# First 256 MLP channels with the tokens stationary, the second tile's root from sums, and boundary adaLN units moved into the MLPs

## The chip, the core and the metric

One core of one Trainium2 chip runs the whole kernel. The metric is device time in microseconds (us), as the median of the runs shown. Engines are named as in the profile: PE multiplies, DVE is the vector engine, ACT the scalar engine, POOL a third engine for small work, SP issues most DMAs.

## The reference, cut to what matters

256 tokens of width 1024 pass four layers. Each layer is a token mixer (attention, convolution, pooling, attention) and then an MLP of 4096 channels. Each of these eight sub-layers does

```python
h = rmsnorm(x, g_pre) * (1 + sc) + sh
y = mixer(h)      # or: square(relu(h @ w1)) @ w2
x = x + gt * rmsnorm(y, g_post)
```

where `sc`, `sh` and `gt` come from `mod = silu(c) @ ada_w[i] + ada_b[i]`, six vectors of 1024 per layer. All is float32, and the products must be good to more than one pass of the fast matmul format.

## The kernel before

**Precision.** Each operand of a large product is split into two planes in the format fp32r: `hi` is the value rounded by ACT (L173 for weights), `lo = value - hi` by DVE (L174). `mm3` (L557, L560, L561) multiplies hi by hi, hi by lo and lo by hi. Weights arrive in tiles of 128x1024 (512 KB): five raw buffers, six `hi` and six `lo` buffers. SP issues their DMAs in the order of the program and waits there when no buffer is free.

**Tokens.** There are two tiles of 128 tokens, t = 0 and 1. The residual stream `xs` has tokens on partitions. Each sub-layer wants `h` transposed: the planes `hT_hi` and `hT_lo`, 128 channels on partitions, eight k by 256 tokens.

**MLP (`ffn`).** There are 16 blocks of 256 channels. For block c, `colblock` multiplies with the weights stationary and all 256 tokens moving (48 matmuls of 128x256 into one PSUM bank); ACT and DVE take relu, square and split it (L609 to L614), and `rowblock` adds its share of `w2` into four banks `y` (24 matmuls of 128x512), one block behind. The last two blocks go tile by tile, t = 0 first.

**Boundary (`boundary`).** Between two sub-layers, for each tile: squares of y (ACT), y times its gain (`y_scaled`, L496), the root (sum and power, L117 to L121, the power on POOL), `residual` (L501), squares of the new x, the second root, scaling (L358 or L388), the transposes on PE, and the fill of the planes (L399, L401 for t = 1; L538, L539 for t = 0). For t = 0 the root goes into the transposes as a diagonal matrix `dg` (L371, L377); for t = 1 it goes into `xa` (L388) ahead of plain transposes (L395). The first two column tiles of `transposed1` are 256 wide, the third 512.

**What sets the order.** A scheduler of the language orders each engine but SP: of what is ready it takes what comes first in the program, and the order is then fixed. `line(engine, ins)` ties the instructions of a boundary into one fixed order on ACT and one on DVE, in program order. `after` keeps casts and subtractions of later weights behind the last fill of the planes (`gate["act"]`, `gate["dve"]`); `gate["free"]` = GFREE = 2 lets the first two loads pass, which are the two weight tiles of the next block 0. A read of a PSUM bank by DVE waits for ACT's read of it.

**adaLN units.** `ada_w` is read in units of 1 MB, 24 per layer. `ada(n)` takes the next n units, in an MLP on DVE (two passes of 128x1024 each, L220 or L222, summed over units and brought to PE by `ada_flush`), elsewhere on PE (L256). Tables `MIX` and `FF` give for each sub-layer: units in its steps, units in the boundary ahead of it, units fetched ahead at its end.

Of the kernel before, what the change touches and what calls it, by code (L numbers as in the profile page):

```python
# [51 lines left out]
def tile_trunk(ctx: ExitStack, tc: tile.TileContext, x, cT, pos, invf, ada_w, ada_bg,  # L52
# [54 lines left out]
    sm.tile([P, 40], F32, tag="align_s", name="align_s", bufs=1)  # L107
# [261 lines left out]
    def transposed0(xa, r):  # L369
        dg = tmp.tile([P, P], F32, tag="dg", name="dg")  # L370
# [40 lines left out]
    def start(hi, lo):  # L411
        def sums(t):
            ms = sm.tile([P, 2], F32, tag="ms", name="ms")
            for n in range(2):
# [89 lines left out]
    def boundary(ys, units, planes=None, tokens=None):  # L504
# [7 lines left out]
        residual(0, v0, rsqrt_eps(*cols(m0)))
        if final:
            nc.sync.dma_start(out[0], xs[:, 0])
        else:
            ms = squares(0)
            xa = scaled(0)
        y_squares(1, ys, 0, m1)
        if not final:
            r = rsqrt_eps(*cols(ms))  # L520
            if tokens is not None:
                tokens(xa, r)
            else:
                bs = transposed0(xa, r)
        v1 = [y_scaled(1, ys, 0)]
        y_squares(1, ys, 1, m1)
        r1 = rsqrt_eps(*cols(m1), eng=V)
        v1.append(y_scaled(1, ys, 1))
        if final:
# [771 lines left out]
```

## Time and profile before

| what | value |
|---|---|
| median of 3 runs | 1192.34 us (1192.28 to 1196.03) |
| profiled execution, its own time | 1196.1 us |
| its span, first to last instruction | 1194.3 us |
| mean granted clock of PE in it | 0.984 |
| PE, DVE, ACT, POOL busy | 1145.1, 843.7, 570.2, 51.9 us |
| instructions | 19384 |
| DMA | 290.13 MB, 243 GB/s on average |

The profiled execution lies at the upper end of the runs. Its time is 1.8 us longer than its span. Busy PE counts matmuls that overlap, so it says only where PE had nothing in flight.

### The profile page before, as it was taken

How to read it: one execution, taken by the hardware profiler on the slowest of the kernel's cores; microseconds unless marked ns; L12 is line 12 of the kernel's file. 1: busy time of each engine (PE TensorE's matmuls, PEld its weight loads, DVE VectorE, ACT ScalarE, POOL GpSimd, SP SyncE). 2: the span in 40 equal slices, each digit the busy share in tenths (PEclk: the TensorE clock that was granted, in tenths of full speed). 3: DMA queues.
4: the chain of work that ended last, by engine and by line, in shares of the span. 5: the costliest groups of instructions: out<-in, count | busy, mean ns of one | idle time of the engine just before them, and what ended most of it. 6: DMA issues, size and time to landing. Idle time of an engine off the chain costs nothing.

```text
span 1194.3 us, 19384 instructions
## 1 busy us (share of the span) xinstructions
PE 1145.1 (96%) x7678; PEld 972.0 (81%) x7678; DVE 843.7 (71%) x1141; ACT 570.2 (48%) x952; POOL 51.9 (4%) x120
## 2 busy tenths in 40 slices
PE   7899989999999999999999989999998999999997
PEld 4667779899878866989898778998967877999996
DVE  3699687877665665868877687777766986655554
ACT  3355564444453245635444463544445665544442
POOL 1000010000010011000000210000010001000000
PEclk9999989999999999999999989999998999999999
DMA  8868757677727785888795577788536432765650
GB/s 336 310 272 326 290 209 299 254 305 290 266 71 251 255 320 194 330 329 345 277 391 213 212 256 285 308 321 325 185 93 228 147 124 87 231 190 182 194 176 36
DMA packets 73390, 290.13 MB, mean 243 GB/s; under 512 B 9986, under 2 KB 15234, under 8 KB 61012
## 3 DMA queue, kind: packets, MB, share of 16 engines
q1 hardware_dynamic: 70484, 280.44, 64.6%
q0 software_dynamic: 2816, 8.46, 2.2%
q8 instruction: 60, 0.98, 0.3%
q14 instruction: 30, 0.25, 0.1%
HBM read 286.57 MB, written 2.29 MB: 242 GB/s over the span
## 4 chain that ended last, share of the span: by engine, by line
PE 58%; DMA 3%; ACT 3%; DVE 3%; issue 2%; POOL 2%; SPq 0%; POOLq 0%; DVEq 0%; ACTq 0%
PE y L557 8%; PE h L557 8%; PE y L560 8%; PE h L561 8%; PE y L561 8%; PE h L560 8%; PE dw_ps L964 2%; ACT junk L135 1%; PE adap L256 1%; PE pw L557 1%; PE pw L560 1%; PE pw L561 1%; POOL r L121 1%; PE s_ps L877 1%; PE hT_ps L395 1%
## 5 line engine op out<-in xcount | busy, mean ns | idle before, releaser
L174 DVE TENSOR_TENSOR lo<-raw,hi 128x1024 fp32r<-128x1024 f32 (+1 forms) x336 | 394.1, 1194 | 168.2 <-ACT hi L173 167.1
L173 ACT CAST hi<-raw 128x1024 fp32r<-128x1024 f32 (+1 forms) x336 | 339.7, 1030 | 278.8 <-PE h L560 123.2
L557 PE MATMUL h<-hT_hi,hi 128*128 128x256 f32 x1024 | 291.9, 285 | 0.0
L560 PE MATMUL h<-hT_lo,hi 128*128 128x256 f32 x1024 | 291.9, 285 | 0.0
L561 PE MATMUL h<-hT_hi,lo 128*128 128x256 f32 x1024 | 291.3, 284 | 0.0
L557 PEld LDWEIGHTS h<-hT_hi,hi 128*128 128x128 f32 x1024 | 198.0, 193 | 3.8 <-issue 0.8
L557 PE MATMUL y<-hi,gh 128*128 128x512 f32 x512 | 200.9, 392 | 0.0
L560 PE MATMUL y<-lo,gh 128*128 128x512 f32 x512 | 200.6, 392 | 0.0
L560 PEld LDWEIGHTS h<-hT_lo,hi 128*128 128x128 f32 x1024 | 198.0, 193 | 2.2
L561 PE MATMUL y<-hi,gl 128*128 128x512 f32 x512 | 199.8, 390 | 0.0
L561 PEld LDWEIGHTS h<-hT_hi,lo 128*128 128x128 f32 x1024 | 197.9, 193 | 0.8 <-issue 0.8
L222 DVE SCALAR_TENSOR_TENSOR acc<-araw,c_act,acc 128x1024 f32<-128x1024 f32 x98 | 120.5, 1279 | 0.0
L561 PEld LDWEIGHTS y<-hi,gl 128*128 128x128 f32 x512 | 96.1, 188 | 23.3 <-issue 2.5
L557 PEld LDWEIGHTS y<-hi,gh 128*128 128x128 f32 x512 | 96.4, 188 | 22.1 <-issue 3.4
L560 PEld LDWEIGHTS y<-lo,gh 128*128 128x128 f32 x512 | 96.4, 188 | 22.0 <-issue 4.2
L609 ACT ACTIVATE r<-h 128x512 f32<-128x512 f32 x64 | 38.0, 594 | 98.0 <-PE h L561 96.8
L612 DVE TENSOR_TENSOR r<-r 128x512 f32<-128x512 f32 x64 | 44.2, 690 | 40.5 <-ACT gh L611 40.5
L496 DVE TENSOR_TENSOR v<-y,bc_g 128x512 f32<-128x512 f32 x32 | 21.8, 687 | 37.0 <-ACT junk L135 24.8
L614 DVE TENSOR_TENSOR gl<-r,gh 128x512 fp32r<-128x512 f32 x64 | 44.2, 691 | 1.7
L611 ACT ACTIVATE gh<-r 128x512 fp32r<-128x512 f32 x64 | 40.6, 634 | 1.7
L256 PE MATMUL adap<-araw,c_act 128*32 128x512 f32 x224 | 34.7, 604 | 3.6 <-DMA araw<-in_ada_w_dram 3.4
L135 ACT ACTIVATE junk<-y 128x512 bf16<-128x512 f32 x32 | 18.9, 592 | 37.5 <-PE y L561 37.3
(255 smaller groups left out, 1466.6 us busy)
## 6 DMA issues: line engine op xcount, KB each, us to landing
raw<-in_w_dram SPq DMA_DIRECT2D x256, 512.0 KB
araw<-in_ada_w_dram SPq DMA_DIRECT2D x96, 1024.0 KB
raw<-in_w_pw_dram SPq DMA_DIRECT2D x24, 512.0 KB
raw<-in_w_o_dram SPq DMA_DIRECT2D x16, 512.0 KB
u<-ud SPq DMA_DIRECT2D x32, 132.0 KB
raw<-in_w_ukv_dram SPq DMA_DIRECT2D x8, 512.0 KB
bc_g<-rowd POOLq DMA_DIRECT2D x8, 512.0 KB, 5.2
bc_a<-rowd POOLq DMA_DIRECT2D x7, 512.0 KB, 4.4
```

What stands on the lines that cost most here:

```text
L135: return A.activation(junk[:, :src.shape[-1]], src, AF.Square, scale=1.0 / math.sqrt(n), accum_out=acc)
L173: put(A.copy(h, raw), "act")
L174: put(V.tensor_tensor(l, raw, h.bitcast(F32), op=ALU.subtract), "dve")
L222: V.scalar_tensor_tensor(acc, raw[:, sl], ck, acc, op0=ALU.mult, op1=ALU.add)
L256: mm = T.matmul(grp["pt"][32 * j:32 * j + 32, :], lhsT, raw[j // 2][:, HALF[j % 2]], start=first, stop=stop)
L557: mm = T.matmul(o, ah, bh, start=start, stop=False, skip_group_check=True)
L560: T.matmul(o, ah, bl, start=False, stop=False, skip_group_check=True)
L561: return T.matmul(o, al, bh, start=False, stop=stop, skip_group_check=True)
L609: A.activation(r, hb, AF.Relu)
L611: A.activation(gh, r, AF.Square)
L612: V.tensor_tensor(r, r, r, op=ALU.mult)
L614: gli = V.tensor_tensor(gl, r, gh.bitcast(F32), op=ALU.subtract)
```

## The change

The change has five parts.

1. `mlp_head`: block 0 of each MLP is computed with the tokens stationary and 256 channels of weights moving, one bank for each token tile, 24 matmuls each. The first tile's (`first(0)`) come in the program inside the boundary, after the first parts of the second tile's planes; the second tile's come at c = 0 in `ffn`. The result has tokens on partitions, so four transposes follow, and the split reads PSUM.
2. `root_ahead`: the sum of squares of the new x of t = 1 is x·x + 2 r x·v + r² v·v, where x·x is kept from the last boundary (`keep_squares`), x·v comes from two `tensor_tensor_reduce` (`cross`) and v·v from two squares on ACT. The squares of the new x now come after the planes, for the next boundary.
3. Order in the boundary: v of the second tile and its first cross product come ahead of the scaling of t = 0; both hi fills of t = 0 come ahead of the second residual, which is split in halves around the scaling of t = 1; the sum for the first root goes to DVE.
4. The adaLN units of the boundaries ahead of MLPs 0, 1 and 2 (1, 4 and 3 units) go to these MLPs' blocks.
5. `dg` has one buffer in place of two; `GFREE` holds only ahead of mixers, since the loads of block 0 come ahead of the boundary.

```diff
+    def keep_squares(t, ms):
+        xx[t] = sm.tile([P, 1], F32, tag="xx", name="xx", bufs=2)
+        G.tensor_scalar(xx[t], ms[:, 0:1], ms[:, 1:2], EPS, ALU.add, ALU.add)
...
-    def transposed1(r, hi, lo):
+    def transposed1(r, hi, lo, rest):
...
         for ks in ((0, 1), (2, 3), (4, 5, 6, 7)):
+            if ks[0] == 4:
+                rest()
...
+    def cross(t, v, n, prev):
+        sl, v = v
+        junk = tmp.tile([P, 512], BF16, tag="junk2", name="junk2", bufs=1)
+        acc = sm.tile([P, 1], F32, tag="xv", name="xv", bufs=4)
+        line("dve", V.tensor_tensor_reduce(out=junk, in0=v, in1=xs[:, t, sl], scale=2.0 / D,
+                                           scalar=prev, op0=ALU.mult, op1=ALU.add, accum_out=acc))
+        return acc
+
+    def root_ahead(t, r, xv, vv):
+        v2 = sm.tile([P, 1], F32, tag="v2s", name="v2s", bufs=2)
+        line("dve", V.tensor_tensor(v2, vv[:, 0:1], vv[:, 1:2], op=ALU.add))
+        a = sm.tile([P, 1], F32, tag="ra1", name="ra1", bufs=2)
+        line("dve", V.tensor_scalar(a, v2, r, xv, ALU.mult, ALU.add))
+        b = sm.tile([P, 1], F32, tag="rb1", name="rb1", bufs=2)
+        line("dve", V.tensor_scalar(b, a, r, xx[t], ALU.mult, ALU.add))
+        r2 = sm.tile([P, 1], F32, tag="r", name="r")
+        gate["pow"] = G.tensor_tensor(r2, b, mhalf, op=ALU.pow)
+        return r2
...
-        residual(0, v0, rsqrt_eps(*cols(m0)))
+        residual(0, v0, rsqrt_eps(*cols(m0), eng=V))
...
+        ms = squares(0)
+        r = rsqrt_eps(*cols(ms))
+        y_squares(1, ys, 0, m1)
+        v1 = [y_scaled(1, ys, 0)]
+        line("act", sq(v1[0][1], D, vv[:, 0:1]))
+        xa = tmp.tile([P, D], F32, tag="xa", name="xa")
+        for h in range(2):
+            line("dve", V.tensor_tensor(xa[:, HALF[h]], xs[:, 0, HALF[h]], bct["a"][:, HALF[h]],
+                                        op=ALU.mult))
+            if h == 0:
+                xv = cross(1, v1[0], 0, 0.0)
+        if tokens is not None:
+            tokens(xa, r)
+        else:
+            bs = transposed0(xa, r)
+        y_squares(1, ys, 1, m1)
+        v1.append(y_scaled(1, ys, 1))
+        r1 = rsqrt_eps(*cols(m1), eng=V)
+        line("act", sq(v1[1][1], D, vv[:, 1:2]))
+        xv = cross(1, v1[1], 1, xv)
...
         if tokens is None:
-            fill0(0)
-        ms = squares(1)
-        r = rsqrt_eps(*cols(ms), eng=V)
+            low = [fill0(h) for h in range(2)]
+        r = root_ahead(1, r1, xv, vv)
+        if tokens is None:
+            low[0]()
+        residual(1, v1[:1], r1)
         if tokens is not None:
+            residual(1, v1[1:], r1)
             tokens(scaled(1), r)
         else:
-            rest = transposed1(r, *planes)
+            rest = transposed1(r, *planes, lambda: residual(1, v1[1:], r1))
             next(rest)
-            fill0(1)
+            low[1]()
+            if first is not None:
+                first(0)
             for _ in rest:
                 pass
+        keep_squares(1, squares(1))
         gate["pool"] = gate["pow"]
-        gate["free"] = GFREE
+        gate["free"] = GFREE if first is None else 0
...
+    def mlp_head(i, h):
         hh, hl = h
+        parts = [load(w1[i, 0, p]) for p in range(2)]
+        banks = []
+
+        def tile_of(t):
+            ts = slice(t * P, (t + 1) * P)
+            b = bank("h", "h0")[:, 0:256]
+            banks.append(b)
+            n = 0
+            for low in (False, True):
+                for kk in range(KT):
+                    wh, wl = parts[kk // 4]
+                    c = slice(256 * (kk % 4), 256 * (kk % 4) + 256)
+                    for st, mv in ((hl, wh),) if low else ((hh, wh), (hh, wl)):
+                        T.matmul(b, st[:, kk, ts], mv[:, c], start=(n == 0), stop=(n == 3 * KT - 1),
+                                 skip_group_check=True)
+                        n += 1
+        return tile_of, banks
...
+                if c == 0:
+                    tile_of(1)
+                    g2 = bank("h", "gT")
+                    for t in range(NT):
+                        rt = r[:, 256 * t:256 * t + 256]
+                        A.activation(rt, banks[t], AF.Relu)
+                        V.tensor_tensor(rt, rt, rt, op=ALU.mult)
+                        for f in range(2):
+                            T.transpose(g2[:, 256 * f + P * t:256 * f + P * t + P],
+                                        rt[:, P * f:P * f + P], ident)
+                    A.copy(gh, g2)
+                    gli = V.tensor_tensor(gl, g2, gh.bitcast(F32), op=ALU.subtract)
...
-        0: ([1, 2, 1, 0, 2, 0, 3, 0, 2, 2, 0, 0, 0, 1, 0, 0], 1, 3),
-        1: ([1, 1, 0, 1, 2, 2, 1, 2, 2, 2, 1, 0, 0, 1, 0, 0], 4, 3),
-        2: ([0, 2, 0, 2, 0, 3, 1, 1, 2, 0, 2, 0, 1, 3, 0, 1], 3, 0),
+        0: ([0, 2, 2, 1, 2, 1, 2, 1, 2, 1, 0, 0, 0, 1, 0, 0], 0, 3),
+        1: ([0, 1, 2, 2, 2, 2, 1, 2, 2, 2, 2, 0, 0, 2, 0, 0], 0, 3),
+        2: ([0, 2, 2, 2, 1, 2, 1, 2, 2, 1, 2, 0, 1, 2, 0, 1], 0, 0),
...
+            first = mlp_head(i, (hi, lo)) if m else None
```

## Rows read from the trace of the kernel before

**Rows 1.** Page, part 1: busy us (share of the span) xinstructions
```profile
PE 1145.1 (96%) x7678; PEld 972.0 (81%) x7678; DVE 843.7 (71%) x1141; ACT 570.2 (48%) x952; POOL 51.9 (4%) x120
```

**Rows 2.** Waits of PE: who, waited for, us in total, times, longest
```profile
PE hT_ps L395 <- DVE xa L388: 11.8, 6, 2.8
...
PE hT_ps L377 <- ACT dg L371: 5.8, 2, 2.9
```

**Rows 3.** Windows, y's end to block 0's relu, MLPs 3, 1, 0, 2: PE, PEclk, DMA
```profile
999.60:1014.00 14.40, 11.85 (x76) 0.88 0.23 75
469.60:485.40 15.80, 12.99 (x108) 1.00 0.86 317
149.80:167.90 18.10, 13.23 (x85) 0.81 0.27 100
685.00:705.90 20.90, 16.77 (x101) 0.76 0.55 190
```

**Rows 4.** Timeline of DVE, boundary ahead of MLP 3: start us, us, what
```profile
994.97 0.69 DVE L496 TENSOR_TENSOR v<-y,bc_g 128x512 f32<-128x512 f32 x1 [2.09 <-ACT junk L135]
996.06 1.41 DVE L501 SCALAR_TENSOR_TENSOR xs<-v,r,xs 128x512 f32<-128x512 f32 x2 [0.39 <-POOL r L121]
...
999.13 0.69 DVE L496 TENSOR_TENSOR v<-y,bc_g 128x512 f32<-128x512 f32 x1 [0.46 <-ACT junk L135]
1000.54 0.21 DVE L117 TENSOR_SCALAR v<-msy 128x1 f32<-128x1 f32 x1 [0.71 <-ACT junk L135]
...
1002.74 0.68 DVE L539 TENSOR_TENSOR hT_lo<-hT_ps,hT_hi 128x512 fp32r<-128x512 f32 x1
...
1004.65 1.54 DVE L388 SCALAR_TENSOR_TENSOR xa<-xs,r,bc_a 128x256 f32<-128x256 f32 x3 [0.66 <-POOL r L121]
1006.11 0.60 DVE L401 SCALAR_TENSOR_TENSOR hT_lo<-hT_ps,shc,hT_hi 128x128 fp32r<-128x128 f32 x2
...
1008.62 1.13 DVE L401 SCALAR_TENSOR_TENSOR hT_lo<-hT_ps,shc,hT_hi 128x128 fp32r<-128x128 f32 x4 [0.73 <-ACT hT_hi L399]
1009.67 4.62 DVE L174 TENSOR_TENSOR lo<-raw,hi 128x1024 fp32r<-128x1024 f32 x4
```

**Rows 5.** Timeline of ACT, the same boundary
```profile
999.53 0.40 ACT L371 ACTIVATE dg<-ident,r 128x128 f32<-128x128 f32 x1 [0.43 <-POOL r L121]
...
1003.02 0.63 ACT L135 ACTIVATE junk<-xs 128x512 bf16<-128x512 f32 x1
...
1007.45 1.14 ACT L399 ACTIVATE hT_hi<-hT_ps,shc 128x128 fp32r<-128x128 f32 x4 [0.27 <-PE hT_ps L395]
1008.46 4.85 ACT L173 CAST hi<-raw 128x1024 fp32r<-128x1024 f32 x5
```

**Rows 6.** Timeline of POOL, the same boundary: the power of the first root
```profile
995.45 0.57 POOL L121 TENSOR_TENSOR r<-v,mhalf 128x1 f32<-128x1 f32 x1
```

**Rows 7.** Timeline of DVE: last fills of the second tile, MLPs 0, 1 and 2
```profile
162.88 1.13 DVE L401 SCALAR_TENSOR_TENSOR hT_lo<-hT_ps,shc,hT_hi 128x128 fp32r<-128x128 f32 x4 [0.73 <-ACT hT_hi L399]
...
481.02 1.13 DVE L401 SCALAR_TENSOR_TENSOR hT_lo<-hT_ps,shc,hT_hi 128x128 fp32r<-128x128 f32 x4 [0.35 <-ACT hT_hi L399]
...
699.92 1.13 DVE L401 SCALAR_TENSOR_TENSOR hT_lo<-hT_ps,shc,hT_hi 128x128 fp32r<-128x128 f32 x4 [0.72 <-ACT hT_hi L399]
```

**Rows 8.** Timeline of DVE, boundary ahead of MLP 0: the first v
```profile
148.98 1.29 DVE L496 TENSOR_TENSOR v<-y,bc_g 128x512 f32<-128x512 f32 x2 [7.70 <-DMA bc_g<-rowd]
```

**Rows 9.** Timeline of DVE, boundary into pooling: tokens of the second tile
```profile
673.16 1.41 DVE L1105 SCALAR_TENSOR_TENSOR xa<-xa,r,shb 128x512 f32<-128x512 f32 x2
```

**Rows 10.** Timeline of PE, boundary ahead of MLP 1: units, then the first tile's products
```profile
469.53 3.64 PE L256 MATMUL adap<-araw,c_act 128*32 128x512 f32 x32
473.10 2.05 PE L377 MATMUL hT_ps<-dg,xa 128*128 128x128 f32 x16
```

**Rows 11.** Page, part 5: busy us, mean ns of one, idle before
```profile
L222 DVE SCALAR_TENSOR_TENSOR acc<-araw,c_act,acc 128x1024 f32<-128x1024 f32 x98 | 120.5, 1279 | 0.0
```

**Rows 12.** Windows: one block of MLP 3; PE, PEld, DVE, ACT, POOL busy, PEclk, DMA
```profile
1020.60:1031.80 11.20, 11.20 (x74) 10.24 (x73) 6.22 (x6) 5.31 (x8) 0.00 (x0) 1.00 0.75 240
```

More of the change, by code (lines that the diff above doesn't have):

```diff
@@ L105, in tile_trunk @@
     A.activation(c_act, ct_in.unsqueeze(2).to_broadcast([P, KT, 32]), AF.Silu)
-    sm.tile([P, 40], F32, tag="align_s", name="align_s", bufs=1)
+    sm.tile([P, 56], F32, tag="align_s", name="align_s", bufs=1)
     HALF = (slice(0, 512), slice(512, 1024))
@@ L352, in squares @@
         return ms
+    xx = {}
+    def keep_squares(t, ms):
+        xx[t] = sm.tile([P, 1], F32, tag="xx", name="xx", bufs=2)
+        G.tensor_scalar(xx[t], ms[:, 0:1], ms[:, 1:2], EPS, ALU.add, ALU.add)
     def scaled(t):
@@ L369, in transposed0 @@
     def transposed0(xa, r):
-        dg = tmp.tile([P, P], F32, tag="dg", name="dg")
+        dg = tmp.tile([P, P], F32, tag="dg", name="dg", bufs=1)
         line("act", A.activation(dg, ident, AF.Copy, scale=r))
@@ L415, in sums @@
                 sq(xs[:, t, 512 * n:512 * n + 512], D, ms[:, n:n + 1])
+            if t == 1:
+                keep_squares(t, ms)
             return rsqrt_eps(*cols(ms))
@@ L424, in root @@
         def root(t, r):
-            dg = tmp.tile([P, P], F32, tag="dg", name="dg")
+            dg = tmp.tile([P, P], F32, tag="dg", name="dg", bufs=1)
             A.activation(dg, ident, AF.Copy, scale=r)
@@ L502, in residual, with boundary @@
                                                op0=ALU.mult, op1=ALU.add))
-    def boundary(ys, units, planes=None, tokens=None):
+    def cross(t, v, n, prev):
[15 more added lines that the diff above has]
+        return r2
+    def boundary(ys, units, planes=None, tokens=None, first=None):
         ada(units)
@@ L508, in boundary @@
         m0, m1 = [sm.tile([P, 2], F32, tag="msy", name="msy") for _ in range(NT)]
+        vv = sm.tile([P, 2], F32, tag="vv", name="vv", bufs=2)
         y_squares(0, ys, 0, m0)
@@ L511, in boundary @@
         v0 = [y_scaled(0, ys, h) for h in range(2)]
-        residual(0, v0, rsqrt_eps(*cols(m0)))
+        residual(0, v0, rsqrt_eps(*cols(m0), eng=V))
         if final:
             nc.sync.dma_start(out[0], xs[:, 0])
[L515 to L529, printed above, removed]
+            y_squares(1, ys, 0, m1)
[3 more added lines that the diff above has]
+            v1.append(y_scaled(1, ys, 1))
             for v in v1:
@@ L533, in boundary @@
             return
-        residual(1, v1, r1)
+        ms = squares(0)
+        r = rsqrt_eps(*cols(ms))
+        y_squares(1, ys, 0, m1)
+        v1 = [y_scaled(1, ys, 0)]
+        line("act", sq(v1[0][1], D, vv[:, 0:1]))
[9 more added lines that the diff above has]
+            bs = transposed0(xa, r)
+        y_squares(1, ys, 1, m1)
+        v1.append(y_scaled(1, ys, 1))
+        r1 = rsqrt_eps(*cols(m1), eng=V)
+        line("act", sq(v1[1][1], D, vv[:, 1:2]))
+        xv = cross(1, v1[1], 1, xv)
         def fill0(h):
@@ L596, in y_banks, with ffn @@
         return [[bank("y", f"y{t}{n}") for n in range(2)] for t in range(NT)]
-    def ffn(i, h, units, ahead, mid):
+    def mlp_head(i, h):
         hh, hl = h
+        parts = [load(w1[i, 0, p]) for p in range(2)]
[14 more added lines that the diff above has]
+        return tile_of, banks
+    def ffn(i, h, units, ahead, mid, first):
+        hh, hl = h
+        tile_of, banks = first
         bcast("g", rows[(i, 1)], 1)
@@ L1190, in tile_trunk @@
             else:
-                head(planes=(hi, lo))
+                head(planes=(hi, lo), first=first and first[0])
             if m:
@@ L1204, in mid @@
                         consts = pool_consts(pool_p, (i + 1) // 3)
-                y = ffn(i, (hi, lo), sched[0], sched[2], mid)
+                y = ffn(i, (hi, lo), sched[0], sched[2], mid, first)
             else:
```

15 lines of the change are left out of this document (8 added, 7 removed).

## The prediction

> **What bounds the kernel now.** I read the page first: PE has something in flight for 1145.1 of 1194.3 us [rows 1], so the time falls only if PE waits less or works less. The waits of PE come next. The largest with one cause are the transposes of the second tile behind `xa` (11.8 us in six boundaries) and the products of the first tile behind `dg` (5.8 us in two) [rows 2]; nothing inside an MLP is on that list. So boundaries are what can be won. [...] Then I read one boundary engine by engine, that ahead of MLP 3, where y ends at 999.60: DVE and ACT run one fixed order, and the reader is to see what DVE does and when it has nothing to do [rows 4, 5].
>
> **The change, step by step, at that boundary.**
>
> *First root.* Today POOL raises it at 995.45 for 0.57 us and `residual` starts at 996.06 [rows 4, 6]. The sum now goes to DVE behind the second v, which ends at 995.66 [rows 4]: 0.21 for the sum, 0.1 and 0.04 for two handovers, 0.57 for the power, so 996.5: +0.4. Where v waits for its gain row from DRAM (7.70 us, MLP 0 [rows 8]; MLP 2 has the like) the root was long done and is now made after v: 0.21 + 0.1 + 0.57 = +0.9.
>
> *`dg`.* ACT makes it at 999.53 [rows 5], after the squares of y's third bank. In the new order the square of v comes ahead of it, and v waits for those squares: v starts at 999.13 + 0.4 and takes 0.65 (0.69 less the overlap), its square 0.75 (0.63 and the accumulator's reading [rows 5]), so `dg` starts at 1000.97: +1.45.
>
> *The last squares of y* follow `dg` on ACT. They ended at 1000.51, since DVE's sum of them starts at 1000.54 [rows 4]; now at 1002.1: +1.6.
>
> *The second root.* From 1002.1 DVE has, in its fixed order: v 0.65, sum 0.13, cross product, three small sums of 0.2, the low plane 0.65 [rows 4], half of the residual 0.71. No row shows `tensor_tensor_reduce`. [...] I take 0.65. The sum is 3.4, so `xa` starts at 1005.5, not 1004.65 [rows 4]: +0.85. The squares that the change takes off this path (two at 0.75, with sum and power) are real, but ACT and DVE spend what they free on v·v, x·v and a later start.
>
> *Second tile's planes.* Three `xa` take 1.54, now with the other residual half (0.71) before the third: they end at 1007.75 where they ended at 1006.19. The first low part is ready at 1008.05, before at 1006.4: +1.65. After it: 0.3, 0.65, 0.60, 1.13 [rows 4], end 1010.65, before 1009.75: +0.9, less than at the start, because today's order waits 0.73 for ACT there.
>
> *Boundaries into mixers* (three). Convolution and attention start their products at the first low part, as nothing of theirs is pulled ahead: +1.65 each. In the pooling boundary the tokens of the second tile end at 674.57 [rows 9], on a DVE line that has no long pause; two cross products and three sums put 1.9 into it: +1.9. Together **+5.2 us**.
>
> *Boundaries into MLPs* (four). Half of block 0, 24 matmuls, moves into the wait. With the second tile's planes complete the other half is nearly done too, for it runs as they come. So block 0 no longer decides; block 1's weights do. Their casts stand behind the last hi fill, which ended at 1008.59 [rows 5], 1.15 before the last low one; today that is hidden by block 0. The new squares for the next boundary stand ahead of those casts in program order: 1.5 us. Then one cast 1.0 and one subtraction 1.2 [rows 4, 5]: block 1 starts 1.5 + 1.0 + 1.2 - 1.15 = 2.55 after the last fill. Last fills today: 164.01, 482.15, 701.05, 1009.75 [rows 4, 7]; new ones +0.9, and 0.45 more ahead of MLPs 0 and 2. Block 1 then starts at 167.9, 485.6, 704.95 and 1013.2; today, by block 0's end, at 167.9, 485.4, 705.9 and 1014.0 [rows 3]: 0, +0.2, -0.95, -0.8, in sum -1.5. The four added transposes of each MLP cost 0.13 apiece at full clock (2.05 for 16 products of that size [rows 10]), half of them while PE waits anyhow: +1.0. Together **-0.5 us**.
>
> *The units.* On PE four of them took 3.64 us [rows 10], in time in which PE would have waited for `dg`: their going gains nothing there, and leaves PE idle for some 4.8 us ahead of MLP 1, whose clock was 1.00. On DVE each costs 2 x 1.28 [rows 11]. A block has 11.20 us of PE and 6.22 of DVE [rows 12], so one unit fits, and two make 11.3: just over. Eight units more give 22 blocks of two over the three MLPs, always with single ones between; the weight buffers and the zeros at the end should cover that. I take 0 and keep +8 for the range (below). Their DMAs stay the same in number; SP meets them one to three blocks later, and DMA is nearly idle in three of the four boundaries (share 0.23 to 0.55 [rows 3]). Single `dg` buffer, `keep_squares`' sum on POOL: 0, since POOL is busy 4% [rows 1].
>
> **Sum:** 5.2 - 0.5 = +4.7 us. The profiled execution took 1196.1 (span 1194.3), 3.8 above the median of the runs shown; it would take 1200.8. Against the median, 1192.34, I predict **1197.0**.
>
> [...] Rows show a DVE instruction with two float32 inputs from SBUF, the residual, at 0.71 for 128x512, about what one with a PSUM input takes [rows 4]. [...]
>
> **Rivals.**
>
> *A. Casts first.* If the scheduler puts block 1's casts ahead of the two new squares, block 1 starts 1.05 after the last fill, 1.5 earlier in four MLPs, as long as block 0 itself is done. For: between squares that share one scratch buffer another instruction may slip in. Against: program order. 4.7 - 6.0 = -1.3: 1191.0.
>
> *B. Faster: the planes of the second tile do not come later.* The place is DVE between v and the last low part; if the earlier root pays for the two cross products (as it would were the last squares of y not held back by `dg`), the last fill stays where it is. Block 1 then starts 1.2 after it (one subtraction): 165.2, 483.35, 702.25, 1010.95, so -2.7, -2.05, -3.65, -3.05; less 2.1 for 16 transposes: -9.3, and mixers 0: 1183.0. Each us that the chain grows costs 7 over seven boundaries, so this holds up to about 1.3 us of growth. For it: DVE has idle time today (0.73 once, 0.66 and 0.71 elsewhere [rows 4]). Against: the sum above.
>
> *C. DVE falls behind in the MLPs.* 22 blocks of two units, each late by the 0.1 above and some 0.25 for ACT's casts: 22 x 0.35 = 7.7: 1204.7. For: 11.3 against 11.2. Against: 98 accumulating passes today [rows 11] and no wait of PE for them.
>
> *D. It does not pull ahead.* If PE's fixed order has the first tile's matmuls behind the second tile's transposes, block 0 ends as late as its planes allow, 0.9 (twice 1.35) later than today: +4.5, +2.1, +5.2: 1204.1.
>
> [...]
>
> **How the numbers follow.** Forecast 0.36, A 0.22, B 0.18, C 0.12, D 0.07, E 0.05. About 0.3% (3.6 us) is what a measurement can tell from no change. Faster: B and 0.06 of A, 0.24. Same: 0.14 of A and 0.10 of the forecast, 0.24. Slower: the rest, 0.52. The range leaves out the better half of B and the upper ends of C, D and E: 1185 to 1205. The forecast alone would be 1193.5 to 1201.
>
> **What would show it.** In the changed profile, ahead of MLP 3: `dg` about 1.4 us after y's end instead of at it; `xa` at 5.9 after it instead of 5.05; cross products near 0.65; two squares between the last hi fill and the first cast; and PE waiting for a low weight tile of block 1. Into the mixers, PE's first products 1.6 us later. In the MLPs no wait of PE for DVE. I am wrong if the last low fill comes no later after y's end than today, if the cast follows the hi fill at once, or if the first tile's matmuls stand behind the transposes.

## The result, and the profile after

The changed kernel takes **1207.78 us** (median of 4 runs, 1206.38 to 1209.56), the kernel before 1192.31 beside it: ratio 1.0108, 95% interval 1.0078 to 1.0137. It is slower by 15.5 us by these medians, where 4.7 was forecast; the ratio sets the loss at 12.9 us (9 to 16), and beside the runs below the kernel before had medians of 1192.9 to 1195.1. The profiled execution took 1209.56 us with a span of 1207.8, 13.5 more than the span of before. Page, part 1, of the changed kernel:

```profile
PE 1145.1 (95%) x7630; PEld 975.9 (81%) x7630; DVE 874.2 (72%) x1211; ACT 579.0 (48%) x984; POOL 56.2 (5%) x120
```

PE has something in flight for as long as in [rows 1], to a tenth of a us, so the 13.5 us are time in which it has nothing. That the two are equal is a balance: eight units, 64 matmuls and some 7.3 us by [rows 10], have left PE, 16 transposes have come, and the other matmuls took longer. The waits of PE, longest groups (who, waited for, us in total, times, longest):

```profile
PE hT_ps L384 <- ACT dg L378: 15.2, 6, 6.9
PE h L608 <- DVE lo L174: 6.5, 7, 1.9
PE hT_ps L404 <- DVE xa L397: 6.4, 4, 3.0
```

Against [rows 2] the wait for `xa` fell from 11.8 to 6.4 us and that for `dg` rose from 5.8 to 15.2. The second line is new: PE waits for low weight planes, four times at block 1 (3.1 us) and three times inside MLPs 1 and 2 (3.4 us). To see where the time goes, I cut each MLP in two: from y's end to the end of block 1 (the boundary and the head), and from there to its own y's end (the interior). Windows of the changed kernel, MLPs 0, 1, 2, 3, two rows each (start:end, us, PE busy, PEld, DVE, ACT, POOL, granted clock, DMA share, GB/s):

```profile
151.20:171.40 20.20, 17.00 (x128) 15.45 (x128) 18.48 (x36) 13.68 (x30) 3.25 (x6) 1.00 0.31 118
171.40:344.02 172.62, 172.62 (x1085) 153.71 (x1088) 127.01 (x128) 81.23 (x102) 2.31 (x5) 1.00 0.76 282
470.85:494.58 23.73, 18.00 (x125) 17.56 (x126) 19.70 (x38) 16.04 (x36) 3.84 (x7) 0.86 0.30 102
494.58:673.85 179.27, 176.57 (x1085) 154.85 (x1087) 141.54 (x144) 80.23 (x95) 3.72 (x5) 0.99 0.80 305
697.77:723.76 25.99, 18.04 (x126) 17.30 (x127) 21.66 (x42) 16.03 (x36) 4.39 (x8) 0.87 0.37 133
723.76:902.49 178.73, 177.15 (x1090) 153.85 (x1089) 139.96 (x142) 79.57 (x102) 2.35 (x5) 1.00 0.76 286
1012.93:1033.13 20.20, 16.99 (x128) 15.44 (x128) 18.48 (x36) 13.76 (x31) 3.25 (x6) 1.00 0.27 97
1033.13:1201.47 168.34, 168.34 (x1056) 152.16 (x1055) 92.49 (x93) 77.74 (x92) 0.56 (x1) 1.00 0.55 172
```

The same cuts of the kernel before, and the mixers from y's end to y's end, give this table (us; the predicted column is what the prediction's sum put there). The differences add up to 13.6, the predictions to 4.7:

| stretch | before | after | difference | predicted |
|---|---|---|---|---|
| attention 0 | 149.80 | 151.20 | +1.4 | 0 |
| MLP 0, boundary and head | 23.82 | 20.20 | -3.6 | +0.25 |
| MLP 0, interior | 172.63 | 172.62 | 0 | 0 |
| convolution | 123.35 | 126.83 | +3.5 | +1.65 |
| MLP 1, boundary and head | 21.47 | 23.73 | +2.3 | +0.45 |
| MLP 1, interior | 173.98 | 179.27 | **+5.3** | 0 |
| pooling | 19.99 | 23.92 | **+3.9** | +1.9 |
| MLP 2, boundary and head | 26.62 | 25.99 | -0.6 | -0.7 |
| MLP 2, interior | 176.47 | 178.73 | **+2.3** | 0 |
| attention 3 | 111.46 | 110.45 | -1.0 | +1.65 |
| MLP 3, boundary and head | 20.10 | 20.20 | +0.1 | -0.55 |
| MLP 3, interior, and the end | 174.63 | 174.67 | 0 | 0 |

An interior in which PE never waits repeats to 0.05 us from run to run (MLP 0: 172.63 before, 172.62 after, 172.60 in e4 and e8), so +5.3 and +2.3 are real. Of the +5.3, though, 1.5 comes and goes: with the same tables the interior of MLP 1 took 177.74 to 177.77 us in e8, e9, e10 and e16 (below), with the same idle time of PE but 1.5 us less of busy time. The window of e8:

```profile
490.77:668.51 177.74, 175.05 (x1084) 153.33 (x1087) 141.82 (x144) 80.67 (x95) 4.17 (x5) 1.00 0.81 308
```

Attention 0 is the same work in all kernels here and lay between 147.9 and 152.9 us in their profiles: its +1.4 says nothing. Boundaries spread by some us, in part with the granted clock (pooling below: 21.64 us at 1.00, 23.92 at 0.86), in part with waits: convolution behind a boundary in the old order took 122.8 us in one kernel and 126.0 in another (e2 and e4 below), both at a mean clock of 1.00.

The boundary ahead of MLP 3, y's end at 1012.93. DVE (start, us, what; CUSTOM_DVE_ANT_0 is the profile's name for the `tensor_tensor_reduce` of `cross`):

```profile
1014.10 0.69 DVE L520 CUSTOM_DVE_ANT_0 junk<-v,xs 128x512 bf16<-128x512 f32 x1
...
1016.04 0.75 DVE L520 CUSTOM_DVE_ANT_0 junk<-v,xs,xv 128x512 bf16<-128x512 f32 x1
...
1017.23 0.27 DVE L528 TENSOR_SCALAR ra<-v2s,r,xv 128x1 f32<-128x1 f32 x1 [0.28 <-POOL r L121]
...
1019.17 0.88 DVE L397 SCALAR_TENSOR_TENSOR xa<-xs,r,bc_a 128x256 f32<-128x256 f32 x2
...
1023.44 1.12 DVE L410 SCALAR_TENSOR_TENSOR hT_lo<-hT_ps,shc,hT_hi 128x128 fp32r<-128x128 f32 x4 [0.30 <-ACT hT_hi L408]
...
1025.86 1.23 DVE L174 TENSOR_TENSOR lo<-raw,hi 128x1024 fp32r<-128x1024 f32 x1 [0.97 <-ACT hi L173]
```

ACT, POOL and PE there:

```profile
1014.25 0.39 ACT L378 ACTIVATE dg<-ident,r 128x128 f32<-128x128 f32 x1
...
1023.27 0.65 ACT L135 ACTIVATE junk<-xs 128x512 bf16<-128x512 f32 x1
...
1024.77 1.06 ACT L173 CAST hi<-raw 128x1024 fp32r<-128x1024 f32 x1
```

```profile
1016.20 0.99 POOL L121 TENSOR_TENSOR r<-v,mhalf 128x1 f32<-128x1 f32 x1 [2.99 <-DVE v L117]
1017.88 0.54 POOL L532 TENSOR_TENSOR r<-rb,mhalf 128x1 f32<-128x1 f32 x1 [0.69 <-DVE rb L530]
```

```profile
1017.28 0.39 PE L663 MATMUL h<-hi,hT_hi 128*128 128x256 f32 x1 [0.54 <-ACT hT_hi L579]
...
1027.14 0.38 PE L608 MATMUL h<-hT_hi,lo 128*128 128x256 f32 x1 [0.76 <-DVE lo L174]
```

The signs are those that the prediction named: `dg` 1.32 after y's end (before 0.07 ahead of it, [rows 5]), `xa` 6.24 after it (before 5.05, [rows 4]), the last fill's end 11.63 (before 10.15), two squares between the last high fill and the first cast, then PE waiting for the low tile of block 1. The first tile's products run from 1017.28, well ahead of the transposes of the second.

And this is MLP 1, DVE and then PE:

```profile
602.76 0.69 DVE L697 TENSOR_TENSOR gl<-r,gh 128x512 fp32r<-128x512 f32 x1
603.37 4.86 DVE L222 SCALAR_TENSOR_TENSOR acc<-araw,c_act,acc 128x1024 f32<-128x1024 f32 x4
608.16 5.76 DVE L174 TENSOR_TENSOR lo<-raw,hi 128x1024 fp32r<-128x1024 f32 x5
```

```profile
609.43 0.39 PE L608 MATMUL h<-hT_hi,lo 128*128 128x256 f32 x1 [1.86 <-DVE lo L174]
```

Two units are four passes, 4.86 us in one piece, and the next block's low planes stand behind them. PE needs the first at 607.57 and gets it at 609.43.

The piece alone does not make the wait. The kernel with the old tables for MLPs 1 and 2 (e7 below) has the same piece, with five low planes behind it, and PE waits nowhere in its interiors:

```profile
589.47 4.87 DVE L222 SCALAR_TENSOR_TENSOR acc<-araw,c_act,acc 128x1024 f32<-128x1024 f32 x4
594.25 5.76 DVE L174 TENSOR_TENSOR lo<-raw,hi 128x1024 fp32r<-128x1024 f32 x5
```

In the changed kernel ACT sat idle ahead of both waits of over 1 us (609.43 in MLP 1, 816.21 in MLP 2) until a relu for which it had to wait, and made the next casts behind that relu:

```profile
600.74 0.60 ACT L694 ACTIVATE r<-h 128x512 f32<-128x512 f32 x1 [8.60 <-PE h L608]
...
805.10 0.60 ACT L694 ACTIVATE r<-h 128x512 f32<-128x512 f32 x1 [8.47 <-PE h L608]
```

So the next high planes were made late, and the four passes stood ahead of their low planes. Whether this is what makes the difference, and whether the order on ACT or the arrival of the weights made them late, was not tried; in the interior of MLP 1 SP waited 69 us for unit buffers, in e7 46 us.

### The profile page after: what moved, and what is told of

It is laid out like the page before. It is cut to its first block, busy times and chain, and to the rows that moved or that the text cites. A ratio compares the mean times of both kernels' runs of the same rounds, so it can differ in the third digit from the quotient of the medians.

```text
span 1207.8 us, 19389 instructions
## 1 busy us (share of the span) xinstructions
PE 1145.1 (95%) x7630; PEld 975.9 (81%) x7630; DVE 874.2 (72%) x1211; ACT 579.0 (48%) x984; POOL 56.2 (5%) x120
## 4 chain that ended last, share of the span: by engine, by line
PE 80%; DVE 9%; ACT 5%; DMA 3%; issue 2%; POOL 1%; SPq 0%; DVEq 0%; POOLq 0%; ACTq 0%
PE y L607 10%; PE y L608 10%; PE y L604 10%; PE h L608 9%; PE h L607 9%; PE h L604 9%; PE adap L256 3%; DVE lo L174 2%; ACT junk L135 2%; PE s_ps L960 2%; PE dw_ps L1047 2%; DVE acc L222 1%; PE pw L604 1%; PE pw L607 1%; PE pw L608 1%
## 5 line engine op out<-in xcount | busy, mean ns | idle before, releaser
L608 PE MATMUL h<-hT_hi,lo 128*128 128x256 f32 x960 | 273.8, 285 | 6.6 <-DVE lo L174 6.5
L604 PE MATMUL h<-hT_hi,hi 128*128 128x256 f32 x960 | 272.6, 284 | 1.3 <-ACT hi L173 1.3
L607 PE MATMUL h<-hT_lo,hi 128*128 128x256 f32 x960 | 272.6, 284 | 0.0
L608 PEld LDWEIGHTS h<-hT_hi,lo 128*128 128x128 f32 x960 | 184.6, 192 | 11.0 <-DVE lo L174 8.5
L604 PEld LDWEIGHTS h<-hT_hi,hi 128*128 128x128 f32 x960 | 184.6, 192 | 6.0 <-ACT hi L173 2.2
L607 PEld LDWEIGHTS h<-hT_lo,hi 128*128 128x128 f32 x960 | 184.6, 192 | 4.7 <-issue 2.5
L222 DVE SCALAR_TENSOR_TENSOR acc<-araw,c_act,acc 128x1024 f32<-128x1024 f32 x114 | 140.0, 1278 | 0.0
L608 PEld LDWEIGHTS y<-hi,gl 128*128 128x128 f32 x512 | 96.2, 188 | 22.3 <-issue 1.7
L121 POOL TENSOR_TENSOR r<-v,mhalf 128x1 f32<-128x1 f32 x27 | 19.0, 705 | 665.3 <-DVE v L117 664.4
L604 PE MATMUL pw<-hT_hi,hi 128*128 128x256 f32 x128 | 37.5, 293 | 0.0
```

Of the source, the lines that this page charges most:

```text
L222: V.scalar_tensor_tensor(acc, raw[:, sl], ck, acc, op0=ALU.mult, op1=ALU.add)
L604: mm = T.matmul(o, ah, bh, start=start, stop=False, skip_group_check=True)
L607: T.matmul(o, ah, bl, start=False, stop=False, skip_group_check=True)
L608: return T.matmul(o, al, bh, start=False, stop=stop, skip_group_check=True)
```

## The experiments

**Which part costs it.** Four kernels: the changed one with the old unit tables; the kernel before with the new tables alone; with the head alone (block 0 by tokens); and with the new order and root alone (`dg` in two buffers). Theory U in these texts blames the units, R the new order with the root from sums.

```diff
# e1: changed kernel      # e2: kernel before (the reverse)
-    FF = {0: ([0, 2, 2, 1, ...], 0, 3), 1: ([0, 1, 2, ...], 0, 3), 2: ([0, 2, 2, ...], 0, 0), ...
+    FF = {0: ([1, 2, 1, 0, ...], 1, 3), 1: ([1, 1, 0, ...], 4, 3), 2: ([0, 2, 0, ...], 3, 0), ...
# e4: kernel before (cut)
+            first = mlp_head(i, (hi, lo)) if m else None
...
# e5: changed kernel, with the old tables (cut)
-            first = mlp_head(i, (hi, lo)) if m else None
...
```

> The changed kernel with the old table of adaLN units (1, 4 and 3 units on PE in the boundaries ahead of MLPs 0, 1 and 2). Theory U (the moved units fill DVE in MLPs 1 and 2 and leave PE idle ahead of MLP 1): the interiors of MLPs 1 and 2, 5.0 and 3.1 us longer in the changed kernel, are as before again, and the 4.6 us of idle PE ahead of MLP 1 is filled: about 9 us less, 1199 us. Rival R (the new order of the boundaries is the cost, and late weights in the MLPs come from their later start): no more than 2 us less, 1206 us.

> The kernel before with the new table of units and nothing else. Theory U: the same 9 us on top of before, 1201 us, with PE waiting for low weight planes in MLPs 1 and 2 behind four accumulating passes of DVE. Rival R: within 2 us of before, since block 0 gives DVE its head start there: 1192 to 1194 us.

> The kernel before with block 0 of the MLPs by tokens (first tile in the boundary) and nothing else: old order, old roots, old units. Theory H (the head start is worth something when the planes come no later and casts stand right behind them): block 1 starts 1.2 us after the last fill, 2 to 3.7 us earlier in four MLPs, less 2 us of transposes: about 1184 us. Rival: block 1 then waits for its own weights, or PE takes the first tile's matmuls after the second tile's transposes: 1190 to 1194 us.

> The changed kernel's boundary (new order, root from sums, both cross products) with the old block 0, the old table of units and two dg buffers. Theory R: the new order alone costs 1.2 to 3.9 us in each of seven boundaries: 1203 us (plus 11). Theory U: the boundaries cost what the first forecast said, 1.65 to 1.9 into mixers and about 0.9 into MLPs: 1201 us at most, and 1197 if a gain row that comes early helps ahead of MLP 0.

| kernel | median us | ratio to before | 95% interval |
|---|---|---|---|
| e1, units undone | 1208.14 | 1.0128 | 1.0090 to 1.0166 |
| e2, units alone | 1202.09 | 1.0061 | 1.0039 to 1.0082 |
| e4, head alone | 1188.32 | 0.9952 | 0.9933 to 0.9971 |
| e5, order and root alone | 1222.07 | 1.0222 | 1.0189 to 1.0256 |

The head gains 6.6 us by the medians, which lies between theory H and its rival. The new order costs some 20 with it (e1 against e4) and 27 without it; 1.8 of the 27 are an effect of addresses (below). That is more than either theory allowed for e5. Most of it lies in the windows from y's end to the end of block 1 (us):

| window | before | e4, head | e5, order | e1, both | changed kernel |
|---|---|---|---|---|---|
| MLP 0 | 23.8 | 22.3 | 27.1 | 27.4 | 20.2 |
| MLP 1 | 21.5 | 22.5 | 26.2 | 23.1 | 23.7 |
| MLP 2 | 26.6 | 20.3 | 30.9 | 26.0 | 26.0 |
| MLP 3 | 20.1 | 18.2 | 22.5 | 20.2 | 20.2 |
| sum | 92.0 | 83.1 | 106.6 | 96.6 | 90.1 |

There the head takes 8.9 us off, and the order puts 14.6 on without the head and 13.5 with it. The tables alone cost 7 (e2, as theory U says), yet taking them out of the changed kernel gives nothing. The windows tell why: in e1 the interiors are back at 173.94 and 176.47, but the window ahead of MLP 0 is 27.38 instead of 20.20, since its gain row lands late again (DVE waits 7.9 us for it, as in [rows 8]). So the tables hold a gain and a loss at different places.

**The tables by MLP.** The old tables for MLPs 1 and 2 only:

```diff
-        1: ([0, 1, 2, 2, 2, 2, 1, 2, 2, 2, 2, 0, 0, 2, 0, 0], 0, 3),
-        2: ([0, 2, 2, 2, 1, 2, 1, 2, 2, 1, 2, 0, 1, 2, 0, 1], 0, 0),
+        1: ([1, 1, 0, 1, 2, 2, 1, 2, 2, 2, 1, 0, 0, 1, 0, 0], 4, 3),
+        2: ([0, 2, 0, 2, 0, 3, 1, 1, 2, 0, 2, 0, 1, 3, 0, 1], 3, 0),
```

> The changed kernel with the old unit tables of MLPs 1 and 2; only MLP 0's table stays new. Theory T (the unit table has two halves: without a unit at the boundary into MLP 0 the gain row lands 4 us sooner and that boundary is about 7 us shorter; with four accumulating passes a block the matmuls of MLPs 1 and 2 wait for DVE): the stretch behind block 1 in MLPs 1 and 2 falls from 179.27 and 178.73 us back to 173.97 and 176.47, and MLP 0's window up to the end of block 1 stays near 20.2; about -7.6 us, 1200. Rival N (the two tables differ by noise, as the whole table undone gave the same time): 1207, and MLP 0's window differs from 20.2 at will.

1202.18 us, ratio 1.0069 (1.0041 to 1.0097). Its windows: MLP 0's head, MLP 1's head, the interiors of MLPs 1 and 2:

```profile
148.97:169.17 20.20, 17.00 (x128) 15.46 (x128) 18.48 (x36) 13.69 (x30) 3.25 (x6) 1.00 0.32 117
...
469.22:492.31 23.09, 19.93 (x158) 16.08 (x158) 19.71 (x39) 15.84 (x36) 3.84 (x7) 1.00 0.78 287
492.31:666.25 173.94, 173.94 (x1085) 153.21 (x1087) 131.94 (x134) 80.52 (x97) 3.42 (x7) 1.00 0.78 298
...
716.17:892.63 176.46, 176.46 (x1090) 153.88 (x1089) 133.60 (x136) 79.50 (x102) 2.35 (x5) 1.00 0.73 274
```

Theory T holds, to 0.05 us in every stretch named; the median fell by 5.6 us of the 7.6. That the tables make MLPs 1 and 2 longer is shown by this; why they do so in a few of their blocks and not in the others is open (above). That the gain row of MLP 0 lands sooner without a unit at that boundary is shown by four kernels (wait 7.7 and 7.9 with it, none without it in the changed kernel and in e2); what in the DMA makes it so was not tried.

**The boundary's chain, one edit at a time**, all on the changed kernel: the new squares behind block 2 (e8), `dg` and the last squares of y ahead of the square of v (e9), the pooling boundary in the old order (e10).

```diff
# e8
-        keep_squares(1, squares(1))
+        if first is None:
+            keep_squares(1, squares(1))
...
+                if c == 2:
+                    last.clear()
+                    keep_squares(1, squares(1))
# e9
-        line("act", sq(v1[0][1], D, vv[:, 0:1]))
...
         y_squares(1, ys, 1, m1)
+        line("act", sq(v1[0][1], D, vv[:, 0:1]))
# e10
+        if tokens is not None:
...
+            residual(1, v1, r1)
+            ms = squares(1)
+            keep_squares(1, ms)
+            tokens(scaled(1), rsqrt_eps(*cols(ms), eng=V))
...
```

> The changed kernel with the squares of the second tile's new x (for the next boundary) behind block 2 of each MLP instead of ahead of the casts of block 1. My prediction's step (the two squares, 1.5 us, stand ahead of block 1's cast in four MLPs): each undisturbed window up to the end of block 1 falls by 1 to 1.5 us from 20.19, in sum -4 to -6, 1202 to 1204. Rival: the casts of block 1 are late for another reason (the last high fill, the weights' DMA): less than 0.5 us per MLP, 1206 to 1208.

> The changed kernel with the square of the second tile's first v moved behind the last squares of y, so that dg and those squares stand where they stood before. Theory O (the new order's cost is the chain: dg +1.4, last squares of y +1.6, second root later): in six boundaries xa and the first low plane come 0.7 to 1 us sooner, mixers' first products 0.7 sooner: -4 to -6 us, 1202 to 1204. Rival D (DVE's own line of v, cross products, sums and the slow power sets the second root, whenever the squares of y come): 0 to -1.5 us, and the root waits for the last square of v instead.

> The changed kernel with the boundary into the pooling sublayer in the old order, its second root from the squares of x. Theory P (there the three small sums of the new root stand between low parts on DVE and behind a square that ACT makes late, so the second tile's tokens come 3.5 us later, not the 1.9 that I priced): the pooling stage falls from 23.9 to about 20 us, -4, 1204. Rival (the stage is set by its transposes at half clock and the gain row's DMA): 22.5 to 24, 1206 to 1208.

**e8**: 1203.20 us, ratio 1.0072 (1.0054 to 1.0090). Windows, MLPs 0 and 3:

```profile
148.12:167.43 19.31, 16.77 (x127) 15.42 (x128) 18.47 (x36) 13.69 (x30) 3.24 (x6) 1.00 0.34 123
...
1005.65:1024.97 19.32, 16.78 (x128) 15.43 (x128) 18.48 (x36) 13.69 (x30) 3.24 (x6) 1.00 0.32 102
```

They are shorter by 0.88 us each, so the squares are on the path, with a little over half the price that I gave them.

**e9**: 1212.40 us, ratio 1.0141 (1.0119 to 1.0164). `dg` is back at 0.31 after y's end, `xa` has not moved (1022.88 - 1016.64 = 6.24), and MLPs 0 and 3 still take 20.18 and 20.19:

```profile
1016.95 0.40 ACT L378 ACTIVATE dg<-ident,r 128x128 f32<-128x128 f32 x1 [0.38 <-POOL r L121]
```

```profile
1022.88 0.88 DVE L397 SCALAR_TENSOR_TENSOR xa<-xs,r,bc_a 128x256 f32<-128x256 f32 x2
```

Rival D holds: a later `dg` costs nothing in these two windows, for DVE sets the second root; its v of the second half starts 2.38 us after y's end in this kernel as in the changed one. That this kernel is slower comes from pooling (28.4 us at a mean clock of 0.71) and convolution (129.9), less 3.0 in the window behind pooling; by how much from the edit is open.

**e10**: 1207.78 us, ratio 1.0112 (1.0088 to 1.0136): no gain. Pooling in the changed kernel, in e8 (same pooling code), and in e10:

```profile
673.85:697.77 23.92, 23.06 (x147) 16.70 (x147) 16.79 (x30) 11.09 (x29) 6.06 (x9) 0.86 0.45 170
```

```profile
668.51:690.15 21.64, 20.15 (x148) 14.78 (x147) 16.70 (x30) 10.97 (x29) 6.07 (x9) 1.00 0.51 186
```

```profile
671.75:697.37 25.62, 24.28 (x147) 19.00 (x146) 17.48 (x28) 9.32 (x25) 5.41 (x10) 0.80 0.54 194
```

The same code took 23.92 at a mean clock of 0.86 and 21.64 at 1.00; the old order took 19.99 at 1.00 in the kernel before and 25.62 at 0.80 here. So the new order costs pooling 1.65 us, close to the 1.9 of the prediction (2.0 beside e2, which has the old order and the new tables and took 19.63 at 1.00), and the rest, 2.3, came with a lower clock in this profile: granted 0.50 from 680 to 686, where the 16 products of 128x128 from 681.91 on took 3.78 us (16 of that size took 2.05 at 1.00 [rows 10]). My theory P, 3.5 by the sums alone, was wrong.

**The cross products.** Taken out (the sum of x times v is left out and put at zero), three times, since the interiors changed as well; e13 and e16 differ from e11 only in padding and in where the zero lies.

```diff
     def cross(t, v, n, prev):
+        return zero
```

> The changed kernel without its two cross products per boundary; it leaves out the sum of x times v, which is put at zero. Theory V (DVE is busy without a pause from the second tile's first v to its last planes, so every instruction there is paid): xa comes 1.4 us sooner after y's end in the MLP boundaries (4.8 instead of 6.2), undisturbed windows fall by 1 to 1.4 us from 20.19, seven boundaries give -8 to -10: 1198 to 1200. Rival A (ACT's squares and the casts set the end): windows fall by less than 0.4 us, 1205.

> The run without the cross products once more (it leaves out the sum of x times v), with the zero that stands for them in the pool of small tiles, so that no other tile changes its address. Theory V (DVE's line is paid in the boundary): with the interiors of the MLPs back at 172.6, 179.3, 178.7 and 168.3 us, what the earlier planes give stands alone: first xa 0.3 to 0.4 us sooner in the MLP boundaries, 3.5 in pooling, 1203. Rival (the interiors stay 1.67 longer, so that the missing products cause it): 1210 to 1212.

> Without the cross products (the sum of x times v is left out), and with the padding of the small tiles such that the MLPs' own tiles lie at a multiple of 512 bytes, as in the changed kernel; in the two runs before this one they lay 64 and 96 bytes short of it, against 0 and 32 of the weight and plane tiles. If that offset masked the price: interiors 172.6, 179.3, 178.7, 168.3; windows up to the end of block 1 19.95; pooling 20.5; in sum -6 to -7 against the changed kernel, 1201 to 1203. Rival: interiors stay 0.4 longer, 1205.

1212.32, 1206.01 and 1206.61 us, ratios 1.0156 (1.0119 to 1.0193), 1.0118 (1.0069 to 1.0166) and 1.0103 (1.0071 to 1.0135). In all three the windows of MLPs 0 and 3 are 19.95, only 0.24 shorter, so theory V was wrong. The interiors of e16 came as expected (172.65, 177.75, 178.74, 168.32); its time did not, since convolution took 131.1 us, 4.2 more than in the changed kernel, for a reason that these runs do not show. In e16, MLP 3, DVE and POOL show what takes the place of the products:

```profile
1012.36 0.69 DVE L507 TENSOR_TENSOR v<-y,bc_g 128x512 f32<-128x512 f32 x1 [0.45 <-ACT junk L135]
...
1013.84 0.16 DVE L532 TENSOR_TENSOR v2s<-vv 128x1 f32<-128x1 f32 x1 [0.67 <-ACT junk L135]
```

```profile
1013.25 0.54 POOL L121 TENSOR_TENSOR r<-v,mhalf 128x1 f32<-128x1 f32 x1 [2.92 <-DVE v L117]
```

DVE now waits for squares of ACT, twice. ACT's line and DVE's are level: taking work from one uncovers the other. In convolution and pooling, where DVE also has rows of the units, the products cost more: in convolution the first matmuls start 8.3 to 8.4 instead of 9.0 us after y's end, and pooling takes 20.48 instead of 21.64.

**Why the interiors changed.** e14 lengthens a padding at the start of the constants by one element, e15 shortens the padding of the small tiles, which lie ahead of the MLPs' own tiles.

```diff
# e14
-    cp.tile([P, 16], F32, name="align_c")
+    cp.tile([P, 17], F32, name="align_c")
# e15
-    sm.tile([P, 56], F32, tag="align_s", name="align_s", bufs=1)
+    sm.tile([P, 24], F32, tag="align_s", name="align_s", bufs=1)
```

> The changed kernel with one padding tile at the start of the constants four bytes per partition longer, nothing else. Theory S (the 1.67 us that every MLP interior was longer by without the cross products is the shift of the weight and plane tiles by four bytes, on TensorE's own instructions): all four interiors 1.67 us longer, 179.27 to 180.9 and so on, 1214 to 1216. Rival: no change, 1207 to 1208.

> The changed kernel with the padding 128 bytes shorter, nothing else, so that the MLPs' tiles lie 128 bytes short of a multiple of 512 while weights and planes lie on one. Theory S2 (the offset between the two kinds of tiles is what the matmuls pay for: 0 gave 0, 64 gave 0.45, 128 gave 1.67 us per MLP): every interior 1.5 to 1.7 us longer, 1213 to 1215. Rival (the longer interiors came with the missing products): no interior changes.

e14: 1209.12 us, ratio 1.0146 (1.0110 to 1.0183), interiors 172.63, 179.25, 178.75, 168.38: unchanged. e15: 1212.98, ratio 1.0162 (1.0117 to 1.0206); its interiors of MLPs 0 and 3:

```profile
169.75:344.06 174.31, 174.31 (x1086) 153.86 (x1088) 127.15 (x128) 80.86 (x102) 2.45 (x5) 1.00 0.75 279
...
1031.27:1201.31 170.04, 170.04 (x1056) 152.24 (x1055) 92.42 (x93) 77.71 (x92) 0.56 (x1) 1.00 0.53 171
```

They are 1.7 us longer, with PE busy throughout and at full clock; MLP 2's is 1.3 us longer, and MLP 1's cannot be read, for it spreads by 1.5 us anyhow. The cost goes with the offset between the MLPs' tiles (`gh`, `gl`, `r`) and the planes and weights, counted modulo 512 bytes by the addresses that the kernels were built with, which the traces do not hold: 0 gave 0 (changed kernel, kernel before, e16, and e14, where all moved by 32 together), 64 gave 0.45 (MLPs 0 and 3 of e13 and e5), 128 gave 1.7 (MLPs 0 and 3 of e15 and e11). Only these offsets were tried, so another count than modulo 512 is not excluded. The offset is 0 in the kernel before and in the changed one, so this is no part of the result; it masked e11, and weighs 1.8 us in e5.

**Together.** Three edits in the changed kernel at once (e7, e8, e10), and the kernel before with the head and MLP 0's table only (e6).

```diff
# e6: kernel before (cut)
...
+            first = mlp_head(i, (hi, lo)) if m else None
-        0: ([1, 2, 1, 0, 2, 0, 3, 0, 2, 2, 0, 0, 0, 1, 0, 0], 1, 3),
+        0: ([0, 2, 2, 1, 2, 1, 2, 1, 2, 1, 0, 0, 0, 1, 0, 0], 0, 3),
```

> The changed kernel with three of the edits tried before taken together: old unit tables in MLPs 1 and 2, the new squares behind block 2, the pooling boundary in the old order. If the costs add by place (units -7.6, squares -3.5, pooling -4 where its transposes do not run at half clock): 1193 to 1195, level with the kernel before, and what remains against it is the second root's later planes into convolution and attention less what the head gives. Rival (they share one cause, so that one edit hides the next): 1199 to 1201.

> The kernel before with two parts of the change: the first 256 channels by tokens, and MLP 0's unit table (no unit at the boundary into it). The old order of the boundary and the old tables of MLPs 1 and 2 stay. Theory S (the parts add where they lie in different places: the head gives 6.6, the gain row of MLP 0 lands before it is needed): MLP 0's window up to the end of block 1 falls from 22.25 in the run with the head alone to 18.2 to 18.7, the value of MLP 3 there; about 1184 to 1185 beside 1195, ratio 0.991. Rival: the wait for the gain row was cover for the second tile's planes, and goes to another wait: ratio 0.995 as with the head alone.

e12: 1194.78 us, ratio 1.0007 (0.9991 to 1.0023), level with the kernel before: the three edits together give back nearly the whole loss. e6: **1185.32 us, ratio 0.9928 (0.9900 to 0.9957)**, faster than both kernels by 8.8 and some 22 us. MLPs 0 and 3 of e6:

```profile
150.55:170.15 19.60, 18.00 (x127) 16.78 (x128) 15.77 (x28) 12.63 (x26) 2.23 (x4) 0.91 0.35 134
...
989.65:1009.27 19.62, 18.02 (x128) 16.80 (x128) 15.78 (x28) 13.47 (x27) 2.23 (x4) 0.91 0.31 106
```

MLP 0 is level with MLP 3, as theory S says, and 2.65 us shorter than in e4, though not at the 18.2 to 18.7 that was expected: both had a mean granted clock of 0.91, where MLP 3 of e4 took 18.15 at 1.00. The two ratios, of e4 and e6, overlap in their intervals, so it is this window and not the total that tells the theory from its rival.

## Why the prediction was wrong

The direction was right; the sum was short by 10.8 us by the medians and by 9.0 by the two profiles, and the result lies beyond the range. The step that failed is the term for the units, put at 0: it measured +7.6 us in the profile, and at least 6.0 in every kernel that has these tables.

- **First root, `dg`, second root: the times near, the path to the second root wrong.** Residual +0.43 (predicted +0.4), `dg` +1.39 (+1.45), `xa` +1.19 (+0.85), last fill +1.48 (+0.9; the terms as written add up to +0.98). The 0.65 of the sum for a cross product was my estimate, which no run shows: the cross products took 0.69 and 0.75, and the nearest row of before, v, has 0.69 for 128x512 [rows 4]. The forecast had the second root wait for the last squares of y behind `dg`; e9 brought both 1 us forward and `xa` did not move, so DVE's own line sets it, and the near hit is luck in this. Of the 0.34 by which `xa` came later than forecast, 0.28 is DVE's wait for POOL's power for the second tile's first root, 0.99 us where [rows 6] show 0.57: it starts at 1016.20, while the cross product runs (1016.04 to 1016.79), and ends at 1017.19. In the other six boundaries it took 0.94 to 1.00 too, and in e16, without the product, 0.54; why it takes longer beside the product is not shown. I had not looked there.
- **But the chain is not one line.** I added the terms as if each us were paid. e9 took 1 us off `dg` and e11, e13, e16 took 1.4 off DVE; the windows moved by 0.0 and 0.24. The prediction's end point in this boundary was near, the price of each term was not.
- **Mixers, +5.2: the start right, the stage not.** First products came 1.5 (convolution) and 1.8 us (attention) later, predicted 1.65; in all four kernels with the old order they start 7.5 and 7.4 us after y's end, in the changed one 9.0 and 9.2. Pooling took 1.65 more at full clock, predicted 1.9. The stages show +3.5, -1.0 and +3.9. In pooling 2.3 us came with the clock, by e8 against the changed kernel; in attention PE was idle 1.1 us longer, but the mean clock rose from 0.95 to 0.98; in convolution 1.7 us are idle PE and 1.8 busy PE, and the spread between profiles is as large.
- **MLP boundaries, -0.5: measured -1.9**, but by other terms, so the near hit is luck. The head took 8.9 off, the new order put 13.5 on, MLP 0's table took 7.2 off and MLP 1's put 0.6 on (e4, e1 and the changed kernel). The forecast had the last fill later by 0.9, and by 1.35 ahead of MLPs 0 and 2; what else the order costs ahead of MLPs 0 and 2, 5 to 6 us each, was not tried apart. Two squares ahead of block 1's cast: 0.88, not 1.5 (e8). MLP 0 gained 3.6, because the gain row landed in time once no unit stood at that boundary; the prediction had named this wait [rows 8] and not asked what the unit's going does to it. MLP 1 lost 2.3: without units PE stood idle for `dg` for 4.6 us, as foreseen, and its clock fell from 1.00 to 0.86; yet with the units back (e7) the window is still 23.09 at a clock of 1.00, so only 0.6 of the 2.3 is theirs in the new order and 1.6 is the order's.
- **The units, 0: this step failed.** "One unit fits, and two make 11.3: just over" was an average over a block, and by the rows it was not even over: four passes in a row take 4.86 us, so 6.22 + 4.86 = 11.08 of 11.20. "Always with single ones between" was not so: the table in the change has four blocks of two in a row, twice, in MLP 1, and three in MLP 2. Interiors grew by 5.3 and 2.3 us, 7.6 together, where the four passes stood ahead of low planes that PE needed; why at two blocks and not at the others is open. "In the MLPs no wait of PE for DVE" was one of the signs; PE waits 1.9 and 1.4 us there for low planes and 0.6 for a high one, and idle PE is 4.3 us in all (2.70 and 1.58, length less busy in the windows). For the rest the same matmuls kept PE busy longer, 176.57 and 177.15 us instead of 173.98 and 176.47, in MLP 1 in part at a lower clock: behind the wait that ends at 609.43 the granted clock was 0.50 from 611 to 614, and products of 128x256 followed each other by 0.21 us instead of 0.12 (mean of the interior 0.99; in e8, at 1.00, PE is busy for 175.05).
- **Rivals.** C, given a chance of 0.12, named the right place, DVE in the MLPs, and its 1204.7 is the forecast with 7.7 on top. That 7.7 is so close to the 7.6 is luck: C has 22 blocks late by 0.35 each, and the trace has two waits of over 1 us, and none in MLP 0 with its five blocks of two. A did not come: the squares stand ahead of the casts. B neither: the planes come later. D neither: the first tile's matmuls ran ahead of the transposes. E, with a chance of 0.05 for slower cross products, neither: the rows have 0.69 and 0.75 beside the 0.65 of the forecast.

C does not exclude the rest of the forecast; it is a term of the same sum, which I left at 0. With it the sum is 12.4, where the profiles have 13.6.

## What to carry to other kernels

When work moves onto an engine that is "nearly full" in its block, do not stop at the block's sum. Look at the longest piece that it puts ahead of what the bottleneck waits for, at whether the planes behind that piece can come late, and at the blocks that follow each other; and ask what clock TensorE has after such a wait (here 0.50 for 3 us behind one of 1.86 us in MLP 1, and 1.00 behind one of 1.43 in MLP 2). Where two engines feed one root in turn, taking work off one of them gains only what the other leaves (here 1.4 us off DVE moved the windows of MLPs 0 and 3 by 0.24); price the pair. And try the parts of a change apart: here one part and one table row of another were worth 8.8 us (e6), and the rest turned that into the loss.

## What was not expected of the hardware

- POOL's power of 128 values took 0.94 to 1.00 us in the seven boundaries where a cross product ran on DVE at its start, and 0.54 without it (e16, ahead of MLP 3).
- Matmuls of an MLP interior took longer when the intermediate's tiles lay off the planes and weights (counted modulo 512 bytes): 64 bytes cost 0.45 us, 128 cost 1.7 of 172.6. Other offsets, and which operand it is, were not tried.
- The same pooling code took 21.64 us at a mean granted clock of 1.00 and 23.92 at 0.86, and the old order 19.99 (kernel before, 1.00) and 25.62 (e10, with other tables, 0.80). What tips it from run to run stays open.
